# Both parts of a split weight in one tile, with a start offset chosen by each use

## The chip, the core and the metric

The kernel runs on one core of one Trainium2 chip. The metric is device time in microseconds (us) of that core, the median of several executions. The core has a matrix engine (TensorE, "PE" in the profile, its weight loads "PEld"), a vector engine (DVE), a scalar engine (ACT), GpSimd (POOL) and a queue for transfers (SP). The engines work from SBUF, which has 128 partitions; TensorE's results go to PSUM. An address in this text is a byte offset within a partition of SBUF.

## What is computed

One decoder layer for 512 tokens of width 2048: a norm, one wide projection, three groups of heads, an output projection added to x, and a last norm.

```python
h = rmsnorm(x, norm_g[l])
proj = h @ w_in[l]
(cv_a, cv_b, cv_gate, fq, fk, fv, f_logit, fox_gate,
 mq, mem_gate) = jnp.split(proj, SPLITS, axis=-1)
...
y_conv = (u @ w_conv_pw[l]) * jax.nn.silu(cv_gate)
...
y_fox = y_fox * jax.nn.silu(fox_gate)
...
y = jnp.concatenate([y_conv, y_fox, y_mem], axis=-1)
x = x + y @ w_out[l]
return rmsnorm(x, final_g)
```

The convolution group and the memory group have 512 channels each, the forgetting attention (fox) has 8 heads of 128. Keys and values of the memory group come from 256 memory tokens and `w_mem_kv`.

## The kernel before

**Products in parts.** Every float32 operand of a product is held as two parts, hi and lo, and a product is three matmuls: hi with hi, hi with lo, lo with hi (`mm3`, lines 102-106). `split` (line 90) makes the parts: ACT copies the source to hi (line 93), DVE subtracts hi from the source and writes lo (line 94).

**Weights.** A weight comes by DMA into a `raw` tile of 4096 bytes per partition (six buffers). `operand` (line 117) splits it into two tiles, `whi` and `wlo`, of 4096 bytes each, three buffers for each. A tile holds eight slices of 128 columns, 512 bytes apart, or two of 512 columns (2048 bytes apart), or four of 256 (1024 bytes apart). `weights` (line 126) does this for a whole weight, in two halves.

**Where a weight is used.** The operand that stays in the array is loaded by a weight load (the *stationary* operand, 128 columns); the other streams through it (the *moving* operand, 256 or 512 columns).

- Start, line 225: memory values. The weight moves, the memory rows `m_hi`, `m_lo` (`mh`, `ml`) are stationary. 512 columns.
- Start, lines 268-273: memory keys. The weight is stationary, `mh`, `ml` move. 256 columns.
- `project` (line 297): 128 features of the wide projection. The weight is stationary, the normed x (`hh`, `hl`) moves, 512 columns, 48 matmuls in a row. It is called 22 times: 8 for the convolution's inputs, 4 for its gates, 4 for the memory queries, 4 for the memory gates, 2 for the first pair of the fox heads.
- Lines 586-591: the convolution's pointwise product. The weight moves, `csh`, `csl` are stationary. 512 columns.
- `pair` (line 710): two blocks of 128 features by seven products of quarters. In `product` (line 727) the weight is stationary and a quarter of the normed x, or a sum of quarters (`s0`, `s1`, `s2`), moves, 256 columns, 24 matmuls for each product. 15 pairs are made so. Three results of a pair are kept in SBUF by ACT (`kept`, line 705, tags p1, p5 and u2, two buffers each) and read by DVE.
- `sides` (line 919), the output projection's plain part: the weight moves, the parts of y (`rs`) are stationary, 512 columns.
- `product` of the output projection (line 975), its part by quarters: the weight moves, `rh` is stationary, 256 columns.

**Order.** Instructions go to the engines in the order in which the program's scheduler sets them; each engine runs its own in order. Attention of one head runs between the products of the next pair, so that transposes and small products stand among the pair's matmuls.

**Addresses.** Tiles of pools on the left are laid out upwards, each rounded to 32 bytes; those on the right lie under the top. The constants stand first, then `raw`, `whi`, `wlo` (pool `wp`), then the pools of the stages.

| tiles | first address | modulo 512 |
|---|---|---|
| constants: ident, mean_r, half_neg, cols, cwt, bf_t, ccol, cb | 16512 | 128 |
| six `raw` | 20480 | 0 |
| three `whi`, three `wlo` | 45056, 57344 | 0 |
| first of a stage's pool on the left: `mh`, then `csh` | 69632 | 0 |
| normed x (`hh`, `hl`), later also the parts `rh` | 163808 | 480 |
| sums `s0` to `s2`, later the parts `rs` | 114656 | 480 |

A constant of few bytes takes a slot of 32: half_neg and bf_t have 4 bytes each and one slot each, cols has 176 bytes in a slot of 192.

Of the kernel before, what the change touches and what calls it, by code (L numbers as in the profile page):

```python
# [10 lines left out]
F32 = mybir.dt.float32  # L11
# [36 lines left out]
def hybrid_layer_kernel(  # L48
# [31 lines left out]
    def nm(s):  # L80
        uid[0] += 1
        return f"{s}_{uid[0]}"
# [7 lines left out]
    def split(hi, lo, src, scale=None):  # L90
        """hi + lo == src (times scale): twelve significant bits each."""
        if scale is None:
            ins = nc.scalar.copy(hi, src)  # L93
            nc.vector.tensor_tensor(lo, src, hi.bitcast(F32), ALU.subtract)  # L94
        else:
            ins = nc.scalar.activation(hi, src, AF.Identity, scale=scale)
            nc.vector.scalar_tensor_tensor(
                lo, src, scale, hi.bitcast(F32), ALU.mult, ALU.subtract
            )
        return ins.ins  # L100
# [15 lines left out]

    def operand(src, out=None):
        """src [P, n, c], whole -> its two parts."""
        if out is None:
            out = tuple(  # L120
                wp.tile(list(src.shape), F32R, tag=t, name=nm(t), bufs=3) for t in ("whi", "wlo")
            )
        split(*out, src)
        return out

    def weights(src, n, c, raw=None, hold=None):
        """src [n * P, c] -> k -> (hi, lo) of its k-th P rows."""
        half = n // 2
        src = src.rearrange("(k p) f -> p k f", p=P)
        parts = []  # L130
        for j in range(2):
            rows = slice(j * half, (j + 1) * half)
            r = raw_tile(half, c) if raw is None else raw[:, rows, :]
            nc.sync.dma_start(out=r, in_=src[:, rows, :])
            parts.append(operand(r, tuple(t[:, rows, :] for t in hold) if hold else None))
        return lambda k: tuple(t[:, k % half, :] for t in parts[k // half])

# [1 line left out]
    ident = const.tile([P, P], F32, name="ident")  # L139
    make_identity(nc, ident)  # L140
    mean_r = const.tile([P, P], F32R, name="mean_r")
    half_neg = const.tile([P, 1], F32, name="half_neg")
    nc.vector.memset(half_neg, -0.5)
    NROW = 2 * KT + 3 * (CW // P)
    cols = const.tile([P, NROW], F32, name="cols")
    cwt = const.tile([P, CW // P, TAPS], F32, name="cwt")
    bf_t = const.tile([NH, 1], F32, name="bf_t")
    ccol = const.tile([P, NT, NH], F32, name="ccol")
    cd = dr.tile([NH, S], F32, name="cd")

    ht = ctx.enter_context(tc.tile_pool(name="ht", bufs=1, side="right", reuse_waits="tile"))
    # x normed, [feature, token], two features' tiles in each
    hs_ = [
# [10 lines left out]

    # ---- start: memory values and keys (rows transposed as they come, their
    # norm applied to the results), x normed and transposed ----
    with tc.tile_pool(name="start", bufs=1) as st:
        m_hi = [st.tile([P, M], F32R, name=f"mh{k}") for k in range(KT)]
        m_lo = [st.tile([P, M], F32R, name=f"ml{k}") for k in range(KT)]
        mean_f = st.tile([P, P], F32, name="mean_f")  # L170
        nc.vector.memset(mean_f, 1.0 / CW)
# [77 lines left out]
        for t in range(MT):  # L249
            nc.vector.tensor_scalar(diag[:, t, :], ident, rsm[:, t : t + 1], None, ALU.mult)  # L250
            split(mv[0][:, t, :], mv[1][:, t, :], os_[t], scale=rsm[:, t : t + 1])
        ones = st.tile([P, P], F32, name="ones")
        nc.vector.memset(ones, 1.0)
        rbc = st.tile([P, M], F32, name="rbc")
        pt = at((P, NROW - KT))
        nc.tensor.transpose(pt, small, ident[: NROW - KT, : NROW - KT])
        nc.vector.tensor_copy(cols[:, KT:], pt)

# [8 lines left out]
        for h in range(NM):  # L267
            wk = weights(w_mem_kv[:, h * P : (h + 1) * P], KT, P)
            load_x(h)
            norm_x(h)  # L270
            o = pj((P, M))
            for k in range(KT):
                mm3(o, wk(k), (m_hi[k], m_lo[k]), k == 0, k == KT - 1)
                if h == NM - 1:
                    x_column(k)
            if h == 0:
                pt = at((P, M))
                for t in range(MT):
                    nc.tensor.matmul(
                        pt[:, t * P : (t + 1) * P], ones, diag[:, t, :], start=True, stop=True  # L280
                    )
                nc.vector.tensor_copy(rbc, pt)
            kt = st.tile([P, M], F32, tag="kt", name=nm("kt"), bufs=1)
            nc.vector.tensor_tensor(kt, o, rbc, ALU.mult)
            split(mk[0][:, h, :], mk[1][:, h, :], kt)
# [11 lines left out]
    def project(f0, per=0):  # L297
        """[P features from f0, tokens] in PSUM."""
        w = weights(w_in[:, f0 : f0 + P], KT, P)
        o = pj()  # L300
        for k in range(KT):
            mm3(o, w(k), (h_hi[k], h_lo[k]), k == 0, k == KT - 1)
        background(per)
        return o

    def silu_of(pool, o, tag, bufs):
        """silu of a PSUM tile."""
        sg = pool.tile([P, S], F32, tag=tag, name=nm(tag), bufs=bufs)
        nc.scalar.activation(sg, o, AF.Sigmoid)
        nc.vector.tensor_tensor(sg, o, sg, ALU.mult)  # L310
        return sg

# [1 line left out]
    NC = CW // P  # L314
    PAD = TAPS - 1
    with tc.tile_pool(name="conv", bufs=1, reuse_waits="tile") as cp:
# [151 lines left out]
        with tc.tile_pool(name="matt", bufs=1, reuse_waits="tile") as ma:  # L468
            # the channel norm's sums and the gates run between the heads
            gates = []  # L470
# [66 lines left out]

        # sums of h's quarters (token halves by feature halves); the last takes
        # the place of the quarter that no product needs
        spool = ctx.enter_context(  # L540
# [55 lines left out]

    # ---- the output projection's operands; what they need of the room of h and
    # its sums falls free with the last pair's products. The convolution's and
    # the memory's parts of y are multiplied as they are; the heads' parts by the
    # same form as the pairs, with sums of their quarters (token halves by halves  # L600
    # of the heads) ----
    NB = D // S
# [55 lines left out]
    def head_ys(j, fa, fb):  # L658
        """Heads j and 4 + j, whole: their quarters' parts and those of the
        sums, which take the room of fa and fb."""  # L660
        base = [room_h(w, j, (2, S)) for w in "hl"]
# [23 lines left out]

# [1 line left out]
    with tc.tile_pool(name="fox", bufs=1, reuse_waits="tile") as fx:  # L687
# [17 lines left out]
        def kept(src, tag):  # L705
            t = fx.tile([P, M], F32, tag=tag, name=nm(tag), bufs=2)
            nc.scalar.copy(t, src)
            return t

        def pair(fa, fb):  # L710
            """Features fa.. and fb.., P each, by Winograd's form of Strassen's
            seven products: the first in PSUM, by token halves, the second in
            SBUF. In three steps, for another pair's to come between."""
            HK = KT // 2
# [8 lines left out]

            # Sums are taken in PSUM: a product adds onto what its bank holds,
            # which copies and an addition have read or changed before. Only a
            # bank's first product starts afresh.
            def product(o, w, a, start=False):
# [159 lines left out]

# [1 line left out]
    head_ys(3, heads[6], last_y)  # L889
    with tc.tile_pool(name="outp", bufs=1, reuse_waits="tile") as op:  # L890
# [3 lines left out]
        gb = op.tile([P, D], F32, name="gb")  # L894
        # by token halves and column blocks
        res = [[op.tile([P, 2, S], F32, name=f"res{h}{n}") for n in range(NB)] for h in range(2)]
# [22 lines left out]
        def sides(n):  # L919
            """y's other parts; the last time, a token tile at a time and to the end."""  # L920
            final = n == NB - 1
# [11 lines left out]
            for j in range(4):  # L933
                hold = tuple(room_h(w, 2 + j, (2, S)) for w in "hl") if final and j >= 2 else None
                ws.append(operand(next_piece(), hold))
                if not final:
                    for t in range(NT):
                        tile_product(os_[t], j, t, ws[j])
                if j == 0:
                    yield  # L940
            for t in range(NT):
                if not final:
                    add(of(t, n), os_[t])
                    continue
                # the very last one by halves, for less to follow its products
                spans = [ALL] if t < NT - 1 else [slice(0, M), slice(M, S)]
# [28 lines left out]
        def product(o, w, name, start=False):  # L975
            wh, wl = operand(w)
            for k in range(HK):
# [102 lines left out]
```

## Time and profile before

| | us |
|---|---|
| median of 3 executions | 870.75 |
| lowest and highest | 870.74 and 870.83 |
| profiled execution, first to last instruction | 868.8 |

For the profiled execution only its span is shown; the median of the timed ones is 1.95 us above it, and that is taken as what lies around the span. In the profile "PE" is the time in which a matmul was under way. The length shown for one matmul is modelled and overlaps the next one's, so what a matmul costs is read from one start to the next. Rows of groups read: line, engine, operation, result and operands (moving first, then stationary), shapes, count, busy us, mean ns of one.

### The profile page before, as it was taken

The numbers are of one execution on the slowest core, as the hardware profiler recorded it, in microseconds if no ns is written. First come the engines' busy times: TensorE is split into PE (matmuls) and PEld (weight loads), VectorE is DVE, ScalarE is ACT, GpSimd is POOL, SyncE is SP. The second block draws the span as 40 slices with busy tenths as digits, with TensorE's granted clock in tenths as the row PEclk, the third lists the DMA queues.
The fourth block names the chain that finished last, engine by engine and source line by source line (L and its number), as shares of the span: only waits on it lengthen the run. The fifth ranks groups of instructions, "written<-read, shape, count | busy, mean of one in ns | idle before, by whom it ended". The sixth has DMA issues, their size and how long they took to land.

```text
span 868.8 us, 14045 instructions
## 1 busy us (share of the span) xinstructions
PE 855.3 (98%) x5562; PEld 775.1 (89%) x5562; DVE 704.8 (81%) x1051; ACT 436.2 (50%) x679; POOL 45.1 (5%) x76
## 2 busy tenths in 40 slices
PE   8999999999999999999999999999999999999996
PEld 6897887888888888999999999999999888998995
DVE  4686799999977998998787878878797886876964
ACT  4874322224346544566565555656464852443523
POOL 1011000000000002010101010101010000000001
PEclk9999999999999999999999999999999999999999
DMA  9972233333332333233434243333334627351415
GB/s 323 356 197 76 70 82 105 97 97 89 94 85 85 109 90 117 79 106 109 121 93 127 74 120 101 107 103 91 107 84 146 239 73 267 97 195 49 146 49 194
DMA packets 143265, 107.52 MB, mean 124 GB/s; under 512 B 3892, under 2 KB 126816, under 8 KB 142560
## 3 DMA queue, kind: packets, MB, share of 16 engines
q1 hardware_dynamic: 141696, 102.52, 39.3%
q0 software_dynamic: 1504, 4.11, 1.3%
q8 instruction: 43, 0.70, 0.3%
q14 instruction: 22, 0.18, 0.1%
HBM read 98.46 MB, written 8.14 MB: 123 GB/s over the span
## 4 chain that ended last, share of the span: by engine, by line
PE 95%; issue 1%; ACT 1%; DVE 1%; DMA 1%; SPq 0%; POOL 0%; POOLq 0%; ACTq 0%
PE pj L732 33%; PE pj L104 13%; PE pj L105 13%; PE pj L106 13%; PE pj L981 8%; PE at L104 3%; PE at L105 3%; PE at L106 3%; PE at L820 1%; DMA raw<-in_w_mem_kv_dram 1%; PE pj L409 0%; PE pj L408 0%; PE pj L262 0%; PE at L262 0%; PE at L782 0%
## 5 line engine op out<-in xcount | busy, mean ns | idle before, releaser
L93 ACT CAST whi<-raw 128x1024 fp32r<-128x1024 f32 x205 | 215.1, 1051 | 324.2 <-PE pj L105 110.9
L94 DVE TENSOR_TENSOR wlo<-raw,whi 128x1024 fp32r<-128x1024 f32 x205 | 250.1, 1221 | 87.5 <-ACT whi L93 86.6
L105 PE MATMUL pj<-hl,whi 128*128 128x512 f32 x352 | 139.6, 397 | 0.0
L106 PE MATMUL pj<-hh,wlo 128*128 128x512 f32 x352 | 139.1, 396 | 0.0
L104 PE MATMUL pj<-hh,whi 128*128 128x512 f32 x352 | 138.9, 396 | 0.0
L732 PE MATMUL pj<-hh,wlo 128*128 128x256 f32 x480 | 135.0, 281 | 0.0
L732 PE MATMUL pj<-hl,whi 128*128 128x256 f32 x480 | 134.9, 281 | 0.0
L732 PE MATMUL pj<-hh,whi 128*128 128x256 f32 x480 | 134.8, 281 | 0.0
L703 DVE TENSOR_TENSOR raw<-raw,raw 128x1024 f32<-128x1024 f32 x76 | 92.7, 1220 | 0.5
L732 PEld LDWEIGHTS pj<-hl,whi 128*128 128x128 f32 x480 | 90.4, 188 | 0.1
L732 PEld LDWEIGHTS pj<-hh,whi 128*128 128x128 f32 x480 | 90.5, 188 | 0.0
L732 PEld LDWEIGHTS pj<-hh,wlo 128*128 128x128 f32 x480 | 90.4, 188 | 0.0
L329 DVE SCALAR_TENSOR_TENSOR acc<-up,cwt,acc 128x512 f32<-128x512 f32 x120 | 85.2, 741 | 0.4
L981 PE MATMUL pj<-whi,rh 128*128 128x256 f32 x448 | 80.0, 280 | 0.7 <-DVE sst L1035 0.4
L104 PEld LDWEIGHTS pj<-hh,whi 128*128 128x128 f32 x352 | 66.1, 188 | 15.9 <-PE pj L262 0.2
L106 PEld LDWEIGHTS pj<-hh,wlo 128*128 128x128 f32 x352 | 66.1, 188 | 15.7
L105 PEld LDWEIGHTS pj<-hl,whi 128*128 128x128 f32 x352 | 66.1, 188 | 15.5
L981 PEld LDWEIGHTS pj<-whi,rh 128*128 128x128 f32 x448 | 68.8, 188 | 1.3 <-DVE res L907 1.1
L981 PE MATMUL pj<-wlo,rh 128*128 128x256 f32 x224 | 62.3, 279 | 0.0
L981 PEld LDWEIGHTS pj<-wlo,rh 128*128 128x128 f32 x224 | 42.1, 188 | 0.2
L796 POOL TENSOR_SCALAR_AFFINE_SELECT b<-b 128x128 f32<-128x128 f32 x32 | 21.3, 676 | 265.6 <-ACT b L795 234.0
L732 PE MATMUL pj<-s0h,whi 128*128 128x256 f32 x120 | 34.9, 291 | 0.0
(302 smaller groups left out, 1720.5 us busy)
## 6 DMA issues: line engine op xcount, KB each, us to landing
raw<-in_w_in_dram SPq DMA_DIRECT2D x104, 512.0 KB, 3.6
raw<-in_w_out_dram SPq DMA_DIRECT2D x32, 512.0 KB, 4.5
raw<-in_w_mem_kv_dram SPq DMA_DIRECT2D x12, 512.0 KB, 7.3
xr<-in_x_dram SPq DMA_DIRECT2D x4, 1024.0 KB, 7.8
res<-in_x_dram SPq DMA_DIRECT2D x8, 512.0 KB, 6.8
out_dram<-res SPq DMA_DIRECT2D x16, 256.0 KB, 2.8
rs<-yd SPq DMA_DIRECT2D x15, 256.0 KB, 4.6
mr<-in_mem_dram SPq DMA_DIRECT2D x8, 256.0 KB, 7.2
```

Source lines behind the costliest of these rows:

```text
L93: ins = nc.scalar.copy(hi, src)
L94: nc.vector.tensor_tensor(lo, src, hi.bitcast(F32), ALU.subtract)
L104: nc.tensor.matmul(o, ah, bh, start=start, stop=False)
L105: nc.tensor.matmul(o, ah, bl, start=False, stop=False)
L106: nc.tensor.matmul(o, al, bh, start=False, stop=stop)
L329: return lambda: nc.vector.scalar_tensor_tensor(a, up[:, j : j + S], cwt[:, c, j : j + 1], a, ALU.mult, ALU.add)
L703: nc.vector.tensor_tensor(o, p, q, ALU.subtract)
L732: nc.tensor.matmul(o, p[:, k, :], q, start=start and k == 0 and i == 0, stop=k == HK - 1 and i == 2, skip_group_check=True,)
L796: nc.gpsimd.affine_select(out=b[:, sl], in_=b[:, sl], pattern=[[-1, P]], compare_op=ALU.is_ge, fill=MASKED, base=0, channel_multiplier=1,)
L820: nc.tensor.transpose(tp[:, (i - j) * P : (i - j + 1) * P], pr[i][:, j * P : (j + 1) * P], ident)
L981: nc.tensor.matmul(o[:, m, :], p, q[:, k, :], start=start and k + m + i == 0, stop=k == HK - 1 and i == 2, skip_group_check=True,)
```

## The change

`operand` makes one tile `wb` of 8704 bytes (two pieces of 4096 and 512 to spare), three buffers, in place of a `whi` and a `wlo`. The two parts stand in it 4096 bytes apart, from an offset that the caller names: 0 (PAIRED), 8 elements or 32 bytes (EVEN), 16 elements or 64 bytes (HEADS). Without a name it is 0. The memory keys, `project` and `sides` name EVEN, the output projection's quarters name HEADS; the pairs, the memory values and the pointwise product keep 0. half_neg and bf_t become two further columns of `cols`; two constants of the start, mean_f and ones, share the buffer of `kt`; the kept results of a pair (p1, p5, u2) have one buffer each. The copy of the small rows into `cols` ends at column NROW.

```diff
+    PIECE = 8 * P
+    PAIRED, EVEN, HEADS = 0, 8, 16
+
+    def operand(src, out=None, off=0):
         if out is None:
+            both = wp.tile([P, 2 * PIECE + P], F32R, tag="wb", name=nm("wb"), bufs=3)
             out = tuple(
-                wp.tile(list(src.shape), F32R, tag=t, name=nm(t), bufs=3) for t in ("whi", "wlo")
+                both[:, o : o + PIECE].rearrange("p (n c) -> p n c", c=src.shape[2])
+                for o in (off, off + PIECE)
             )
         split(*out, src)
...
-    def weights(src, n, c, raw=None, hold=None):
+    def weights(src, n, c, raw=None, off=0):
...
-            parts.append(operand(r, tuple(t[:, rows, :] for t in hold) if hold else None))
+            parts.append(operand(r, off=off))
...
-    half_neg = const.tile([P, 1], F32, name="half_neg")
+    NROW = 2 * KT + 3 * (CW // P)
+    cols = const.tile([P, NROW + 2], F32, name="cols")
+    half_neg, bf_t = cols[:, NROW : NROW + 1], cols[:NH, NROW + 1 : NROW + 2]
     nc.vector.memset(half_neg, -0.5)
-    NROW = 2 * KT + 3 * (CW // P)
-    cols = const.tile([P, NROW], F32, name="cols")
     cwt = const.tile([P, CW // P, TAPS], F32, name="cwt")
-    bf_t = const.tile([NH, 1], F32, name="bf_t")
...
-        mean_f = st.tile([P, P], F32, name="mean_f")
+        mean_f = st.tile([P, M], F32, tag="kt", name="mean_f", bufs=1)[:, :P]
...
-        ones = st.tile([P, P], F32, name="ones")
+        ones = st.tile([P, M], F32, tag="kt", name="ones", bufs=1)[:, :P]
...
-            wk = weights(w_mem_kv[:, h * P : (h + 1) * P], KT, P)
+            wk = weights(w_mem_kv[:, h * P : (h + 1) * P], KT, P, off=EVEN)
...
-        w = weights(w_in[:, f0 : f0 + P], KT, P)
+        w = weights(w_in[:, f0 : f0 + P], KT, P, off=EVEN)
...
-            t = fx.tile([P, M], F32, tag=tag, name=nm(tag), bufs=2)
+            t = fx.tile([P, M], F32, tag=tag, name=nm(tag), bufs=1)
...
-                ws.append(operand(next_piece(), hold))
+                ws.append(operand(next_piece(), hold, EVEN))
...
-            wh, wl = operand(w)
+            wh, wl = operand(w, off=HEADS)
```

More of the change, by code (lines that the diff above doesn't have):

```diff
@@ L115, in raw_tile @@
         return wp.tile([P, n, c], F32, tag="raw", name=nm("raw"), bufs=6)
-    def operand(src, out=None):
+    PIECE = 8 * P
+    PAIRED, EVEN, HEADS = 0, 8, 16
+    def operand(src, out=None, off=0):
         if out is None:
+            both = wp.tile([P, 2 * PIECE + P], F32R, tag="wb", name=nm("wb"), bufs=3)
             out = tuple(
-                wp.tile(list(src.shape), F32R, tag=t, name=nm(t), bufs=3) for t in ("whi", "wlo")
+                both[:, o : o + PIECE].rearrange("p (n c) -> p n c", c=src.shape[2])
+                for o in (off, off + PIECE)
             )
@@ L256, in hybrid_layer_kernel @@
         nc.tensor.transpose(pt, small, ident[: NROW - KT, : NROW - KT])
-        nc.vector.tensor_copy(cols[:, KT:], pt)
+        nc.vector.tensor_copy(cols[:, KT:NROW], pt)
         def x_column(k):
```

## The prediction

> **What bounds the kernel now.** First the page: the span, the engines' shares, and the chain of work that ended last.
>
> ```profile
> span 868.8 us, 14045 instructions
> ...
> PE 855.3 (98%) x5562; PEld 775.1 (89%) x5562; DVE 704.8 (81%) x1051; ACT 436.2 (50%) x679; POOL 45.1 (5%) x76
> ...
> PEclk9999999999999999999999999999999999999999
> ...
> PE 95%; issue 1%; ACT 1%; DVE 1%; DMA 1%; SPq 0%; POOL 0%; POOLq 0%; ACTq 0%
> PE pj L732 33%; PE pj L104 13%; PE pj L105 13%; PE pj L106 13%; PE pj L981 8%; PE at L104 3%; PE at L105 3%; PE at L106 3%; PE at L820 1%; DMA raw<-in_w_mem_kv_dram 1%; PE pj L409 0%; PE pj L408 0%; PE pj L262 0%; PE at L262 0%; PE at L782 0%
> ```
>
> TensorE is never long idle, at full granted clock, and 95% of the chain is matmuls. Next, whom TensorE waits for (total us, times, longest), first and last of seven rows, and the stretches where DVE might be near:
>
> ```profile
> PE pj L104 <- ACT mh L96: 2.4, 1, 2.4
> ...
> PE pj L732 <- DVE wlo L94: 0.2, 1, 0.2
> ```
>
> ```profile
> 150.00:240.00 90.00, 90.00 (x408) 73.24 (x407) 83.09 (x127) 28.79 (x45) 0.58 (x1) 1.00 0.33 91
> ...
> 525.00:570.00 45.00, 45.00 (x375) 44.74 (x374) 37.58 (x56) 26.83 (x44) 2.83 (x5) 1.00 0.38 106
> ```
>
> TensorE waits for a few us in all. DVE (third busy time) has 6.9 of 90 us free in the convolution and 7.4 of 45 in a head's stage. So the time is the number of matmuls times the distance from one start to the next, and the change can only act through that distance, or by making an operand late.
>
> **The distance is not the same everywhere.** Rows of the timeline, 512 moving columns: `project` first, then the pointwise product, then `sides` with a weight moving, then the end of `sides`, where the weight lies in the room of h. Each fence has the first row of an unbroken stretch and the first row behind it.
>
> ```profile
> 98.06 0.40 PE L106 MATMUL pj<-hh,wlo 128*128 128x512 f32 x1
> ...
> 103.66 0.40 PE L106 MATMUL pj<-hh,wlo 128*128 128x512 f32 x1
> ```
>
> ```profile
> 315.41 0.39 PE L104 MATMUL pj<-csh,whi 128*128 128x512 f32 x1
> ...
> 326.31 0.40 PE L104 MATMUL pj<-hh,whi 128*128 128x512 f32 x1
> ```
>
> ```profile
> 787.09 0.40 PE L104 MATMUL pj<-whi,rs 128*128 128x512 f32 x1
> ...
> 792.69 0.40 PE L104 MATMUL pj<-whi,rs 128*128 128x512 f32 x1
> ```
>
> ```profile
> 845.98 0.39 PE L104 MATMUL pj<-rh,rs 128*128 128x512 f32 x1
> ...
> 848.72 0.40 PE L105 MATMUL at<-wlo,rs 128*128 128x512 f32 x1
> ```
>
> Distances: 5.60 us over 24 matmuls, **233.3 ns**; 10.90 over 48, **227.1**; 5.60 over 24, **233.3**; 2.74 over 12, **228.3**. Now 256 columns: pairs and quarters of the output projection as merged pieces of the chain (start, us, what), memory keys from the timeline.
>
> ```profile
> 518.77 13.84 PE pj L732 x117
> ...
> 736.31 14.01 PE pj L981 x120
> ```
>
> ```profile
> 47.01 0.28 PE L105 MATMUL pj<-ml,whi 128*128 128x256 f32 x1
> ...
> 48.45 0.28 PE L105 MATMUL pj<-ml,whi 128*128 128x256 f32 x1
> ```
>
> **118.3 ns** for a pair's matmul, **116.75** for the quarters, and 1.44 us over 12, **120.0**, for the keys. Put these beside the addresses. Let D be the stationary operand's address less the moving one's, modulo 512; slices of all these tiles lie multiples of 512 apart, so D is one number for a whole stage.
>
> | columns | D = 0 | D = +32 | D = -32 |
> |---|---|---|---|
> | 512 | 227.1 (csh, w), 228.3 (rh, rs) | 233.3 (`project`) | 233.3 (`sides`) |
> | 256 | 120.0 (keys) | 118.3 (pairs) | 116.75 (quarters) |
>
> The rows at the end of the pointwise product:
>
> ```profile
> 325.63 0.39 PE L104 MATMUL pj<-csh,whi 128*128 128x512 f32 x1
> 325.86 0.39 PE L105 MATMUL pj<-csl,whi 128*128 128x512 f32 x1
> 326.09 0.39 PE L106 MATMUL pj<-csh,wlo 128*128 128x512 f32 x1
> ```
>
> Starts here are 226 to 227 ns apart (0.68 us over three, with the row at 326.31 above): a stream at D = 0 settles at 226.7, and the mean of 227.1 holds a slow beginning. What could carry it shows where weight loads stand beside matmuls:
>
> ```profile
> 683.98 0.28 PE L732 MATMUL pj<-s2l,whi 128*128 128x256 f32 x1
> 683.98 0.19 PEld L732 LDWEIGHTS pj<-s2h,wlo 128*128 128x128 f32 x1
> ```
>
> The load for the next matmul begins with the matmul ahead of it, so two reads of SBUF run side by side. I choose to read D as the cause, because two quite different streams at D = 0 agree.
>
> **The change part by part.** Two slots of 32 bytes go from the constants (cols grows from 176 to 184 bytes, still 192), so `raw` begins at 20480 - 64 = 20416, `wb` at 20416 + 6 x 4096 = 44992, which is 448 modulo 512; 8704 is 17 x 512, so all three buffers are. With its offset a weight is at 448 (PAIRED), 480 (EVEN) or 0 (HEADS). Pools behind begin at 44992 + 3 x 8704 = 71104, also 448. Tiles on the right stay. Hence:
>
> - `project`: weight 480, h 480, D from +32 to 0.
> - `sides`: weight 480, y 480, D from -32 to 0.
> - pairs: weight 448, h and sums 480, D from +32 to -32.
> - keys: weight 480, `mh` 448, D from 0 to +32.
> - values, pointwise product, output quarters, the last `rh` weights: D as before.
>
> Counts are from the groups by shape; of like rows one stands for the others (three of 352, three of 56 and three of 52, three of 64; for the pairs three of 480 and nine of 120).
>
> ```profile
> L104 PE MATMUL pj<-hh,whi 128*128 128x512 f32 x352 | 138.9, 396 | 0.0
> ...
> L732 PE MATMUL pj<-hh,whi 128*128 128x256 f32 x480 | 134.8, 281 | 0.0
> ...
> L732 PE MATMUL pj<-s0h,whi 128*128 128x256 f32 x120 | 34.9, 291 | 0.0
> ...
> L104 PE MATMUL at<-whi,rs 128*128 128x512 f32 x56 | 20.8, 395 | 0.0
> ...
> L104 PE MATMUL pj<-whi,rs 128*128 128x512 f32 x52 | 20.0, 400 | 0.6 <-ACT whi L93 0.6
> L104 PE MATMUL pj<-mh,whi 128*128 128x256 f32 x64 | 18.8, 293 | 0.0
> ```
>
> 1. `project`: 1056 matmuls. 48 in a row, as in the pointwise product, so its 227.1, settling included: 1056 x 6.2 = **6.5 us**. Bounds: 0, and 6.6 ns each (7.0) if settled throughout.
> 2. `sides`: 324 matmuls, in runs broken by output quarters, so the short run's 228.3: 324 x 5.0 = **1.6 us**. Bounds 0 and 2.1.
> 3. Pairs: 15 x 7 x 24 = 2520 matmuls, 118.3 - 116.75 = 1.54 ns each: **3.9 us**. The trace has no pair at D = -32; the quarters are its nearest row (same columns, same order of parts). Bounds: 120.0, the dearest row of 256 columns, a loss of 4.3; and 3.9.
> 4. Keys: 192 matmuls from 120.0 to the pairs' 118.3: **0.3 us**.
> 5. Smaller products whose tiles shift by 64 bytes against the right side (memory attention, forget logits: some 100 matmuls) get a D that no long stream here shows. At 3 ns each either way that is 0.3 us; I take 0.
>
> Nothing is added to an engine: the same copies and subtractions are made. The kept results lose a buffer. In ACT's and DVE's timelines:
>
> ```profile
> 469.25 0.39 ACT L707 COPY p<-pj 128x256 f32<-128x256 f32 x1
> ...
> 491.71 0.36 ACT L707 COPY p<-pj 128x256 f32<-128x256 f32 x1
> ```
>
> ```profile
> 482.12 0.41 DVE L700 TENSOR_TENSOR col<-pj,p 128x256 f32<-128x256 f32 x1
> ```
>
> p5, written at 469.25, is last read by 482.53, and the next pair's copy comes at 491.71: 9.2 us to spare, so the second buffer is worth nothing. If that cover went, ACT's queue behind the copy (a pair's next hi copies) would wait, and TensorE with it. The hi part's slot now comes free only with the lo part's last matmul, one matmul (0.12 or 0.23 us) later. DVE's and TensorE's rows show the lead of an operand, here the shortest in this head's stage:
>
> ```profile
> 497.39 1.21 DVE L94 TENSOR_TENSOR wlo<-raw,whi 128x1024 fp32r<-128x1024 f32 x1
> ```
>
> ```profile
> 500.58 0.28 PE L732 MATMUL pj<-s2h,wlo 128*128 128x256 f32 x1
> ```
>
> 500.58 - 498.60 = 1.98 us, sixteen matmuls, so I cost it at 0. TensorE's saving is 12.3 us, 1.4%: DVE's 83.1 us then stand in 88 us instead of 90, still with room. The constants that share `kt` are written before the stage's waits begin; nothing there. Sum: 6.5 + 1.6 + 3.9 + 0.3 = **12.3 us**. The span goes from 868.8 to 856.5; with the 1.95 us between span and median, 858.4.
>
> **A rule against it.** The streams above differ by 6 ns of 233 with D while the weight load runs beside the matmul. The Trainium skill (TensorE: Matmul & The Clock Gate, Step-by-step: what each phase is for) says that TensorE has two independent read ports into SBUF and that "Loading the next tile's weights doesn't steal SBUF read bandwidth from the running matmul." By that rule no address could matter, the sum would be 0 and the time 870.75; the trace's 227.1 beside 233.3 does not agree with it.
>
> **Rivals.**
>
> - *D is not the cause.* The fast streams would owe their distance to something else: where the results go, what other engines do. For: the D = 0 sample of 512 columns is only some 100 quiet matmuls. Against: two stages with different neighbours agree, and so does the reversed order at 256 columns. Time: 870.7. This is also the case in which the change does not do what it says. The page's rule above would have it so. Chance 7%.
> - *Only the 512-column streams gain.* The quarters' 116.75 might belong to their results, which go to two halves of a bank by turns, not to D. Then 12.3 - 3.9 = 8.4 us, 862.3. Chance 10%.
> - *The pairs land on the keys' level*, 120.0: 8.4 - 4.3 = 4.1 us, 866.6. Chance 2%.
> - *Operands come late: slower.* One tile frees both parts together, so each hi copy starts a matmul later. Were there no lead, each operand would hold TensorE for that: 105 of pairs x 0.12, 60 of 512 columns (44 of `project`, 16 of `sides`) x 0.23, 28 of the quarters x 0.12 = 29.8 us, less the 12.3: 888. It decides where an operand's lead falls under one matmul; with 1.98 us in the rows it would need ACT or DVE to lag by a whole subtraction more. Chance 4%.
> - Forecast as summed, 858.4: 77%.
>
> **How the numbers follow.** The likeliest is 858.4. Its own uncertainty is the settling of broken streams (up to 2 us less gain) and a different order of instructions among attention and pairs (1 to 2 us either way); the only sure further gain is 0.5 + 0.5 us from settled streams in steps 1 and 2. With the second rival taken in, the range is 856.0 to 863.0. Faster or slower by 0.2% (1.7 us) is about what a measurement of this kernel can tell from no change: faster 0.77 + 0.10 + 0.02 = 0.89, same 0.07, slower 0.04.
>
> **What would show it.** In the timeline after, `project` should run at 227 ns a matmul once settled and `sides` near 228; a chain piece of L732 should have 116.7 ns for each matmul (117 in 13.66 us, not 13.84); L981 should stay at 116.75, and the keys leave 120. DVE and ACT copies should keep their length. I am wrong if `project` stays at 233, if L732 stays at 118 or rises, or if TensorE's list of waits gains rows for hi or lo parts.

## The result and the profile after

| | before | after |
|---|---|---|
| median, us (4 executions each) | 870.76 | 860.78 |
| lowest and highest | 870.74, 870.83 | 860.14, 860.89 |
| span of the profiled execution | 868.8 | 859.0 |

The ratio is 0.9883, with a 95% interval from 0.9869 to 0.9897: 10.0 us less, where 12.3 were forecast (858.4 us). The profiled execution took 860.89 us, 1.9 us more than its span, as before.

First a correction. The text ahead of the prediction says that in the convolution's pointwise product the weight moves and `csh`, `csl` are stationary. It is the other way round, as the rows show (the moving operand stands first): `csh` and `csl` move. D is 0 either way, and no number hangs on it.

The page of after: span, busy times, granted clock in tenths over 40 slices, and the chain by engine (in the rows further on, line 732 is now 739 and 981 is 988).

```profile
span 859.0 us, 14010 instructions
...
PE 844.9 (98%) x5562; PEld 773.0 (90%) x5562; DVE 703.7 (82%) x1051; ACT 435.6 (51%) x679; POOL 46.6 (5%) x76
...
PEclk8999999999999999999999999999999999999999
...
PE 95%; ACT 2%; issue 1%; DVE 1%; DMA 1%; SPq 0%; POOL 0%; ACTq 0%; POOLq 0%
```

The same 5562 matmuls still fill 98% of a shorter span, and DVE and ACT are busy as long as before; of the granted clock, only the first of 40 slices is lower (8, where before had 9). So the time went out of the distance from matmul to matmul. Timeline rows of after, `project` and then `sides`, each a matmul and the 24th behind it:

```profile
118.05 0.39 PE L104 MATMUL pj<-hh,wb 128*128 128x512 f32 x1
...
123.49 0.39 PE L104 MATMUL pj<-hh,wb 128*128 128x512 f32 x1
```

```profile
777.70 0.39 PE L104 MATMUL pj<-wb,rs 128*128 128x512 f32 x1
...
783.14 0.39 PE L104 MATMUL pj<-wb,rs 128*128 128x512 f32 x1
```

Both are 5.44 us over 24: 226.7 ns, where the same stages had 233.3. Now merged pieces of the chain of after, three of the pairs and one of the quarters (start, us, what):

```profile
395.78 13.66 PE pj L739 x117
...
421.84 13.90 PE pj L739 x118
...
440.96 13.31 PE pj L739 x114
...
727.04 14.02 PE pj L988 x120
```

Per matmul: 116.75, 117.8, 116.75 and 116.8 ns. The first and third are the forecast's level; the second is a level between that and the 118.3 of before. The memory keys in the timeline, a matmul and the 21st behind it:

```profile
46.85 0.28 PE L105 MATMUL pj<-ml,wb 128*128 128x256 f32 x1
...
49.33 0.28 PE L105 MATMUL pj<-ml,wb 128*128 128x256 f32 x1
```

2.48 us over 21, 118.1 ns, where it was 120.0. All distances added up from start to start, over the whole trace, by class:

| matmuls | before, us | after, us | difference | forecast |
|---|---|---|---|---|
| `project`, 1056 | 247.31 | 241.12 | -6.19 | -6.5 |
| `sides`, 324 | 75.97 | 74.29 | -1.68 | -1.6 |
| pairs, 2520 | 302.18 | 299.51 | -2.67 | -3.9 |
| memory keys, 192 | 23.98 | 23.76 | -0.22 | -0.3 |
| quarters, 672 | 79.74 | 79.89 | +0.15 | 0 |
| memory values, 96 | 24.91 | 26.05 | +1.14 | 0 |
| transposes, 266 | 29.30 | 28.71 | -0.59 | 0 |
| attention, 264 | 42.17 | 42.36 | +0.19 | 0 |

The first four rows give 10.76 of the 12.3 us; the lower four take 0.89 back. What is left, 9.87, is the span's 9.8. Last, whom TensorE waits for in after (total us, times, longest), whole:

```profile
PE pj L104 <- ACT mh L96: 2.3, 1, 2.3
PE at L184 <- POOL ident masks.py:199: 1.4, 1, 1.4
PE pj L104 <- ACT wb L93: 1.2, 1, 1.2
PE pj L988 <- DVE res L914: 0.7, 2, 0.4
PE at L241 <- DMA mr<-in_mem_dram: 0.4, 1, 0.4
```

No weight of `project` or of a pair is in it. The one row for a weight is at the turn from the fox heads to the output projection, a single wait of 1.2 us where before had one of 0.6 there (`ACT whi L93`) and one of 0.2 for a pair's `wlo` just ahead. In the table it lies in the row of pairs, since it follows the last pair's last matmul, and takes some 0.2 us from their gain.

### The profile page after: what moved, and what is told of

It is laid out like the page before. It is cut to its first block, busy times and chain, and to the rows that moved or that the text cites. A ratio compares the mean times of both kernels' runs of the same rounds, so it can differ in the third digit from the quotient of the medians.

```text
span 859.0 us, 14010 instructions
## 1 busy us (share of the span) xinstructions
PE 844.9 (98%) x5562; PEld 773.0 (90%) x5562; DVE 703.7 (82%) x1051; ACT 435.6 (51%) x679; POOL 46.6 (5%) x76
## 4 chain that ended last, share of the span: by engine, by line
PE 95%; ACT 2%; issue 1%; DVE 1%; DMA 1%; SPq 0%; POOL 0%; ACTq 0%; POOLq 0%
PE pj L739 33%; PE pj L104 13%; PE pj L105 13%; PE pj L106 13%; PE pj L988 8%; PE at L104 3%; PE at L105 3%; PE at L106 3%; PE at L827 1%; DMA raw<-in_w_mem_kv_dram 1%; ACT wb L93 0%; PE pj L415 0%; PE pj L416 0%; PE pj L269 0%; PE at L789 0%
## 5 line engine op out<-in xcount | busy, mean ns | idle before, releaser
L93 ACT CAST wb<-raw 128x1024 fp32r<-128x1024 f32 x205 | 215.4, 1052 | 246.1 <-PE pj L106 73.2
L94 DVE TENSOR_TENSOR wb<-raw,wb 128x1024 fp32r<-128x1024 f32 x205 | 250.0, 1221 | 64.2 <-ACT wb L93 60.3
L739 PE MATMUL pj<-hh,wb 128*128 128x256 f32 x960 | 177.3, 280 | 0.0
L739 PEld LDWEIGHTS pj<-hh,wb 128*128 128x128 f32 x960 | 150.1, 188 | 0.0
L104 PE MATMUL pj<-hh,wb 128*128 128x512 f32 x352 | 137.3, 391 | 0.1
L105 PE MATMUL pj<-hl,wb 128*128 128x512 f32 x352 | 137.4, 391 | 0.0
L106 PE MATMUL pj<-hh,wb 128*128 128x512 f32 x352 | 137.2, 390 | 0.0
L739 PE MATMUL pj<-hl,wb 128*128 128x256 f32 x480 | 134.2, 280 | 0.0
L739 PEld LDWEIGHTS pj<-hl,wb 128*128 128x128 f32 x480 | 90.2, 188 | 0.0
L988 PE MATMUL pj<-wb,rh 128*128 128x256 f32 x672 | 80.2, 280 | 0.7 <-DVE res L914 0.7
L988 PEld LDWEIGHTS pj<-wb,rh 128*128 128x128 f32 x672 | 79.5, 188 | 1.4 <-DVE res L914 1.1
L104 PEld LDWEIGHTS pj<-hh,wb 128*128 128x128 f32 x352 | 66.1, 188 | 14.0 <-PE pj L269 0.3
L106 PEld LDWEIGHTS pj<-hh,wb 128*128 128x128 f32 x352 | 66.1, 188 | 13.7
L105 PEld LDWEIGHTS pj<-hl,wb 128*128 128x128 f32 x352 | 66.1, 188 | 13.5
```

Source lines behind the costliest of these rows:

```text
L104: nc.tensor.matmul(o, ah, bh, start=start, stop=False)
L105: nc.tensor.matmul(o, ah, bl, start=False, stop=False)
L106: nc.tensor.matmul(o, al, bh, start=False, stop=stop)
L739: nc.tensor.matmul(o, p[:, k, :], q, start=start and k == 0 and i == 0, stop=k == HK - 1 and i == 2, skip_group_check=True,)
L988: nc.tensor.matmul(o[:, m, :], p, q[:, k, :], start=start and k + m + i == 0, stop=k == HK - 1 and i == 2, skip_group_check=True,)
```

## The experiments

Each edit below is made to the kernel after the change, except where it says the kernel before. "Settled" is the mean distance in a run of matmuls of equal D, without its first nine. Each timed kernel has its own executions of the kernel before beside it; they had medians of 870.6 to 871.1.

### Is it D, or the rest of the change?

The rest first: one tile, moved constants, single buffers for kept results, but all offsets equal, so that D of `project`, `sides` and the pairs is again that of before.

```diff
-    PAIRED, EVEN, HEADS = 0, 8, 16
+    PAIRED, EVEN, HEADS = 16, 16, 16
...
-    def operand(src, out=None, off=0):
+    def operand(src, out=None, off=PAIRED):
...
-    def weights(src, n, c, raw=None, off=0):
+    def weights(src, n, c, raw=None, off=PAIRED):
```

> The changed kernel with one offset of 64 bytes for every weight: the merged tile, the moved constants and the single buffers of the kept results stay, but weights lie at 0 modulo 512 and h at 480, as before, so D is +32 for project and the pairs and -32 for sides and the output quarters. If D alone sets the spacing: project 233.3 ns, pairs 118.3 ns, time 870 to 871.5 us, no change against before. If the merged tile or another order of instructions brought part of the gain, the time lies below 869 us.

Measured: 870.91 us (10 executions), ratio 0.9998 (0.9989 to 1.0007). `project` took 247.35 us and the pairs 302.08, as before. Two small stages do move here, since weights and the tiles behind them shift against each other: the keys get D = +64 and the pointwise product too, 23.14 us and 11.21 (before 23.98 and 10.90). Pieces of the pairs in this kernel's chain:

```profile
402.01 13.85 PE pj L739 x117
...
428.35 13.96 PE pj L739 x118
```

They are 118.4 and 118.3 ns, the level of before. The wait at the turn to the output projection is 1.1 us here, so its growth comes with the one tile and not with D. The second kernel goes the other way: the kernel before, with its two tiles and two buffers, and 448 bytes more in the constants, which put `whi` and `wlo` at 448 modulo 512. D of pairs becomes -32 and D of quarters +32; `project` and `sides` swap their signs, -32 and +32.

```diff
-    cols = const.tile([P, NROW], F32, name="cols")
+    cols = const.tile([P, NROW + 112], F32, name="cols")
...
-        nc.vector.tensor_copy(cols[:, KT:], pt)
+        nc.vector.tensor_copy(cols[:, KT:NROW], pt)
```

> The kernel before with 448 bytes of spare constants and nothing else: its separate tiles lie at 448. D: project -32, pairs -32, sides +32, output quarters +32, keys 0. If D is the cause, the pairs go from 118.3 to 116.9 ns (about 3 us less, as measured for the change), the quarters from 116.75 to 118.3 (1 us more), project and sides stay at 233.3: 868.0 to 869.5 us. If the pairs gained from the merged tile, nothing falls: 870.7 or, with the quarters' loss, 871.8.

Measured: 868.88 us (8 executions), ratio 0.9975 (0.9965 to 0.9986). Its chain, a piece of pairs and one of quarters:

```profile
427.36 13.66 PE pj L732 x117
...
732.68 14.21 PE pj L981 x120
```

These pairs run at 116.75 ns (some short runs at 117.8) and the quarters at 118.4, an exchange of the two levels of before (118.3 and 116.75). Pairs fall from 302.18 to 298.92 us, quarters rise from 79.74 to 80.56, and `project` and `sides` stay to the hundredth (247.31 and 75.97). Moving the weights and the pools behind them by 448 bytes, with no instruction changed but the length of a copy's target, moves the time. Together the two kernels show that the offset acts, and that the tile, the constants and the buffers together are worth nothing that 0.1% could show.

### Where the slower start comes from

The memory values lost 1.14 us. One suspect is `raw`, which now begins at 448 modulo 512; here it is back at a multiple of 512, and so is `wb`, with offsets that keep each named D but that of the keys, which becomes -32.

```diff
-    PAIRED, EVEN, HEADS = 0, 8, 16
+    PAIRED, EVEN, HEADS = 112, 120, 0
...
-    cols = const.tile([P, NROW + 2], F32, name="cols")
+    cols = const.tile([P, NROW + 18], F32, name="cols")
...
-            wh, wl = operand(w)
+            wh, wl = operand(w, off=PAIRED)
```

> The changed kernel with 64 bytes of spare constants, so that raw, wb and the stages' pools begin at 0 modulo 512 again, and offsets of 448, 480 and 0 that keep every D of the change (the memory keys go from +32 to -32). If the slower start of the changed kernel (memory values 26.0 us in place of 24.9, transfer packets of 512 bytes at 33 ns in place of 27 in the first 40 us) comes from raw tiles at 448, it returns to 27 ns and the time falls by about 1 us more for the start and 0.3 for the keys, to 859.5. If it is chance between executions, the time stays at 860.5 to 861 (0.3 less for the keys).

Measured: 859.88 us (4 executions), ratio 0.9869 (0.9855 to 0.9884), which overlaps with the change's own interval. The memory values still took 25.94 us. Packets of 512 bytes in the first 40 us did get shorter, 27.4 ns in the mean against 33 in the kernel after (27.1 before), but the values gained nothing, so that suspect falls. The table of windows shows what stands beside the loss (us, then busy us and matmuls of PE, PEld, DVE, ACT, POOL, granted clock, DMA share, GB/s): 10 to 15 us in before, in after, and in this kernel.

```profile
10.00:15.00 5.00, 5.00 (x21) 4.02 (x21) 3.81 (x6) 2.36 (x4) 0.00 (x0) 0.73 1.06 408
```

```profile
10.00:15.00 5.00, 5.00 (x14) 3.89 (x14) 3.68 (x6) 2.04 (x3) 0.00 (x0) 0.50 1.05 389
```

```profile
10.00:15.00 5.00, 5.00 (x14) 3.85 (x14) 3.98 (x7) 2.21 (x3) 0.00 (x0) 0.50 1.05 407
```

Where TensorE was granted half of its clock it did 14 matmuls in these 5 us; at 0.73 it did 21. In the half-clock stretch most of the values' matmuls stand 427 ns apart, behind it some 230. The later kernel with D = 256 and +64 (below) has the same instructions and addresses in this stage as the kernel after, and its profile shows this:

```profile
10.00:15.00 5.00, 5.00 (x22) 3.98 (x21) 4.07 (x7) 2.62 (x4) 0.00 (x0) 0.77 1.05 389
```

Its values took 24.61 us. So the 1.14 us are not the change's doing: like kernels had 24.6 and 26.05 by the clock that they were granted. The distances are the surer sign: the kernel with one tile and the old offsets shows a granted clock of 1.00 in these 5 us, yet its matmuls stand 427 ns apart up to 13.8 us. Why one execution is granted more than another was not tried.

### How the distance depends on D

To see the relation whole, each of the 22 calls of `project` and each of the 15 pairs got its own D (at_d turns a D into an offset in elements).

```diff
+PROJ_D = (0, 64, 96, 128, 160, 192, 224, 256, 288, 320, 352, 384, 416, 448, 16, 8, 4, 496, 504, 508, 48, 464)
+PAIR_D = (64, 96, 128, 160, 192, 224, 256, 288, 320, 352, 384, 416, 448, 16, 496)
...
+    at_d = lambda d: (d + 32) % 512 // 4
+    proj_off = deque(at_d(d) for d in PROJ_D)
...
-        w = weights(w_in[:, f0 : f0 + P], KT, P, off=EVEN)
+        w = weights(w_in[:, f0 : f0 + P], KT, P, off=proj_off.popleft())
...
-                wh, wl = operand(w)
+                wh, wl = operand(w, off=off)
```

> Each call of project and each pair takes its own offset, so that D runs through 0 to 480 in steps of 32, with a few finer ones, in one execution. If D modulo 512 is a relation between two reads that run side by side, the spacing is a smooth or stepped function of D with 226.7 at 0 and 233.3 at +32 and -32 for 512 columns, and 116.7 at -32 for 256. If D = 0 and D = -32 are special only by chance, the spacing shows no order in D. A D that is better than those of the change would show below 226.7 or below 116.7.

The same with a finer choice:

```diff
+PROJ_D = (256, 252, 248, 244, 240, 260, 264, 272, 276, 280, 12, 16, 20, 24, 500, 496, 488, 184, 192, 200, 208, 72)
+PAIR_D = (64, 56, 72, 48, 80, 60, 68, 52, 320, 216, 232, 220, 228, 224, 40)
```

> As the scan by 32, with finer steps: project at 256 and 4 to 24 bytes around it, at 12 to 24, near -16, and at 184 to 208; pairs at +64 and 4 to 24 around it, at 320 and at 216 to 232. If the relation has a period of 256, 240 and 272 give what -16 and 16 gave (settled 228.5 and 226.7 ns), 248 and 264 what -8 and 8 gave (233.3 and 230.6). If the period is 512, they differ. A level under 226.7 or 116.6 would be a better place for the operands.

Measured: 867.4 and 868.11 us, one execution each; most of their streams run at a slow D. Settled distances at 512 columns, each D beside the one 256 bytes on:

| D and ns | D + 256 and ns |
|---|---|
| 0: 226.7 in the kernel after; 227.2 and 229.2 in the first scan's first call, in short runs | 256: 226.7 |
| 4: 232.3 | 260: 232.4 |
| 8: 230.6 | 264: 230.7 |
| 16: 226.7 in one kernel, 233.4 in the other | 272: 233.4 |
| 64: 233.4 | 320: 233.4 |
| 96: 234.2 | 352: 234.2 |
| 192: 228.9 | 448: 229.0 |
| 240: 228.3 | 496: 228.5 and 227.7 |
| 244: 233.3 | 500: 233.3 |
| 252: 226.7 | 508: 226.7 |

Timeline rows behind two of these, D = 256 in the first scan (5.44 us over 24) and D = 260 in the second (5.59 us over 24):

```profile
156.44 0.39 PE L108 MATMUL pj<-hh,wb 128*128 128x512 f32 x1
...
161.88 0.39 PE L108 MATMUL pj<-hh,wb 128*128 128x512 f32 x1
```

```profile
134.00 0.40 PE L108 MATMUL pj<-hh,wb 128*128 128x512 f32 x1
...
139.59 0.39 PE L108 MATMUL pj<-hh,wb 128*128 128x512 f32 x1
```

Four bytes more than 256 cost 6 ns a matmul; four bytes less cost nothing. The relation returns after 256 bytes, not after 512, and no D went below 226.7. In the scans only the weight moves, so by them alone its own address could be what counts. The pointwise product decides that: with the weight at 0 and `csh` at 0 it settled at 226.7 ns in the kernel before; with the weight at 0 and `csh` at 448 (D = +64), in the kernel with one tile and the old offsets, it took this for 24 matmuls:

```profile
317.21 0.39 PE L104 MATMUL pj<-csh,wb 128*128 128x512 f32 x1
...
322.81 0.39 PE L104 MATMUL pj<-csh,wb 128*128 128x512 f32 x1
```

That is 5.60 us, 233.3 ns, the level of D = 64 in the scan: it is the distance between the two operands that counts. At 256 columns the levels reach from 113.4 to 120.4 ns: D = 64 had 113.4 in the second scan and 116.6 in the first, 320 had 116.9, 52 had 116.8, 192 and 448 both 117.8, 160 and 416 both 120. For D = 64 the chains of the two kernels show it in the same first pair, first scan and then second:

```profile
347.13 11.31 PE pj L747 x96
```

```profile
347.99 10.89 PE pj L747 x96
```

117.8 and 113.4 ns, with the same operands and addresses, but another D in the `project` calls ahead. So D doesn't fix the distance alone; a stream can settle at more than one level.

### Is there a better D?

The scans offer +64 for the pairs, and 256 in place of 0 for `project` and `sides`:

```diff
-        w = weights(w_in[:, f0 : f0 + P], KT, P, off=EVEN)
+        w = weights(w_in[:, f0 : f0 + P], KT, P, off=72)
...
-                wh, wl = operand(w)
+                wh, wl = operand(w, off=24)
...
-                ws.append(operand(next_piece(), hold, EVEN))
+                ws.append(operand(next_piece(), hold, 72))
```

> The changed kernel with other offsets: project and sides at D = 256 in place of 0, pairs at D = +64 in place of -32; all else as in the change. In the scan, D = 256 stood at 226.7 ns from its second matmul on and +64 at 116.6. If the relation has a period of 256 bytes, D = 256 is the same as 0 and settles as slowly: project stays at 228.3 ns on average, and only the pairs can gain, from 117.1 to 116.6 (1.3 us): 859.5. If D = 256 settles at once, project and sides gain some 1.5 us more: 858. If +64 was good by chance of its place in the scan, the pairs stay at 117.1 and the time at 860.8.

Measured: **856.10 us** (4 executions), ratio 0.9835 (0.9819 to 0.9852), whole below the change's interval. `project` took 241.09 us and `sides` 74.33: D = 256 is D = 0. The pairs took 295.82, 3.7 us less than with -32, and their chain has both levels again, 117.8 and 113.4 ns:

```profile
438.93 13.43 PE pj L739 x114
...
464.67 13.38 PE pj L739 x118
```

The profiled span fell by 4.9 us (859.0 to 854.1): 3.7 are the pairs', and 1.4 those of the values of the start (24.61 against 26.05), which are not the edit's; other stages lost 0.2. In the next kernel `project` and `sides` got the D = 16 that had run at 226.7 in the first scan, with pairs at +64 (offsets 12, 4 and 24 for the calls of the diff above).

> The changed kernel with project and sides at D = 16 in place of 0 and pairs at +64 in place of -32. In the scan D = 16 settled at 226.7 ns, as 0 does. If broken streams settle sooner there, project falls under 228.3 ns on average and the time under 859.5; if 16 is the same as 0, 859.5 by the pairs alone; if settling hangs on chance, project spreads to 230 and the time is 860 to 861.

Measured: 863.26 us (4 executions), ratio 0.9915 (0.9901 to 0.993). `project` took 246.54 us, 233.5 ns in the mean, and `sides` 75.45: the fast D = 16 of the scan was a matter of its place. The call that had run at 226.7 ns there did so again (227.0), and so did the second call, 226.7; nearly all others settled at 233. The pairs kept their gain (295.41). The last kernel for the time: the fastest so far, and +64 at the keys and the quarters also.

```diff
-            wk = weights(w_mem_kv[:, h * P : (h + 1) * P], KT, P, off=EVEN)
+            wk = weights(w_mem_kv[:, h * P : (h + 1) * P], KT, P, off=16)
...
-            wh, wl = operand(w, off=HEADS)
+            wh, wl = operand(w, off=120)
```

> The kernel of e5 (project and sides at D = 256, pairs at +64) with the output quarters and the memory keys at +64 too, in place of -32 and +32. If +64 is the better place for any stream of 256 columns, the quarters fall from 116.8 to about 115.5 ns and the keys from 118.3 to 115.5: 672 x 1.3 + 192 x 2.8 = 1.4 us, 854.7. If it is good only for the pairs' order of results, the time stays at 856.1.

Measured: 855.87 us (4 executions), ratio 0.9826 (0.981 to 0.9843). Quarters went from 79.77 to 79.05 us and keys from 23.76 to 23.29: 1.2 us of the 1.4 that were expected. The time shows little of it, since the values of the start took 25.54 us in the profiled execution, against 24.61. Against the kernel with pairs alone at +64 the intervals overlap, so the two can't be told apart; both beat the change.

### Which meeting is the costly one?

If one reading of a tile collided with one loading, giving the hi and the lo part of a `project` weight different D should slow one place of the three matmuls only. By turns hi had 0 and lo 244, and hi -12 and lo 0 (`low` is the lo part's own offset).

```diff
+    turns = deque([(8, 69), (5, 8)])
...
-        w = weights(w_in[:, f0 : f0 + P], KT, P, off=EVEN)
+        hi_off, lo_off = turns[0]
+        turns.rotate(1)
+        w = weights(w_in[:, f0 : f0 + P], KT, P, off=hi_off, low=lo_off)
```

> The changed kernel with the two parts of project's weights at different D, by turns: one call with hi at 0 and lo at 244, the next with hi at -12 and lo at 0 (alone, 0 settles at 226.7 ns, 244 and -12 stand at 233.3). Matmuls run hi, hi, lo, and a load runs beside the matmul ahead of it. If the load beside a matmul is what it meets, the distance behind the second matmul (lo is loaded beside it) differs from the others in each call: the long one in the first kind of call, the short one in the second. If a matmul's own stationary operand counts, it is the third. If the distances do not hang on single meetings but on the state of the whole stream, no place stands out.

Measured: 860.51 us, one execution. Mean distances behind the first, second and third matmul of `mm3`: 227.7, 228.2 and 227.5 ns in one kind, 227.5, 228.8 and 228.7 in the other. These means mix two sorts of calls. Fourteen of the 22, of both kinds, settled at 226.7 to 226.8, as this one with hi at -12 and lo at 0:

```profile
110.20 0.39 PE L104 MATMUL pj<-hh,wb 128*128 128x512 f32 x1
...
115.64 0.39 PE L104 MATMUL pj<-hh,wb 128*128 128x512 f32 x1
```

Five settled at 231 to 232. In triples that took 690 to 705 ns the places differ: 232.1, 234.6 and 230.9 ns in the first kind, 229.7, 233.4 and 233.5 in the second. A long second place in the first kind fits "the load beside a matmul", a short first place in the second kind fits neither reading. So the same two D give a fast or a slow stream, and the 233.3 that -12 (500 or 244) gave where both parts had it is not a price of single matmuls: the distance seems to hang on the state of the whole stream. What collides inside the chip these runs don't settle: that stays open.

## Why the prediction was right, and where its sizes were off

- **What bounds the kernel** was read rightly: with no engine's work changed, 10 us went out of matmul distances, and TensorE's share stayed at 98%.
- **D is the cause:** right. The tile without the offsets gave 870.91 us, and the offset without the tile gave 868.88. The rival by which D does nothing, 870.7, falls. The Trainium skill (TensorE: Matmul & The Clock Gate, Step-by-step: what each phase is for) says that loading the next weights takes no read bandwidth from the running matmul. As the prediction read that rule, 860.78 and 870.91 us, from kernels that differ in the offsets, would have to be one time; that reading doesn't hold here, though no run shows that read bandwidth is what is lost.
- **Modulo 512** was too much said: three values of D could not show a period. The scans show 256.
- **`project` and `sides`:** 6.19 and 1.68 us for 6.5 and 1.6. Both settle at the 226.7 named; `project`'s mean was 228.3, not 227.1 (before, 234.2 and not 233.3), since some of its 22 calls are broken by other work and settle anew.
- **Pairs** are the mis-sized term: 2.67 us for 3.9. The step took the quarters' 116.75 for every pair's matmul. The pairs settle at two levels, 116.75 and 117.8, and matmuls in undisturbed runs had 117.1 in the mean: that is some 1.0 of the 1.2 us that are missing, and the longer wait at the turn is the other 0.2. The 116.75 was true of quarters and of the kernel before moved by 448 (3.26 us there), so D = -32 can give it; the stream in the new kernel does so in some of its pieces only. With the weights' base at 0 and the same D the pairs took 298.75 us, so the level depends on more than D.
- **Keys and quarters:** as forecast (118.4 and 116.8 ns settled). The keys' D became +32, as worked out.
- **Single buffers and later slots at nothing:** nearly right. No wait for a part of a pair's or `project`'s weight came, and the change without its D lost nothing clear of noise, so the rival of late operands falls. But the wait at the turn grew from 0.6 and 0.2 us to 1.2, and to 1.1 with the one tile and the old D; the kernel before moved by 448 bytes still had 0.6 and 0.3. The sum had no term for it.
- **Only 512 columns gain** falls: the kernel before moved by 448 gained 2.2 us with `project` unchanged. Pairs on the keys' level falls too.
- **The start** was not in the sum: 1.1 us lost in the profiled execution to a lower granted clock, which other kernels with the same start did not lose.

The forecast's 12.3 less 1.5 (the four terms: 1.2 from pairs, 0.3 from `project`) less 0.9 (the rest of the table) is 9.9; the span fell by 9.8. The direction rested on two streams at D = 0 that agreed; the size of the 256-column term rested on one other stage, and that is the one that was off.

## What to carry to other kernels

When TensorE is the bound and its matmuls follow one another without gaps, compare the start-to-start distance of stages with the same shape: a difference of 2 or 3% between them may be the distance between the two operands' addresses and can be had by an offset alone, with no instruction changed. Try the offset by a scan within one kernel, one value for each call, and confirm the best in a kernel that uses it throughout, since a value that was fast at one place (16 here) can be slow at most others. Use a level from another stage as a bound, not as a price.

## What the runs showed of the hardware that was not expected

- The distance repeats with 256 bytes of D, and 4 bytes can matter: 226.7 ns at 252 and 256, 232.4 at 260 (512 columns).
- Equal addresses are among the best for 512 columns but not for 256: there +64 reached 113.4 ns, +32 118.3, and 256 (the same as 0) 120.0.
- A stream settles at one of several levels with the same D: 113.4 and 117.8 ns within one kernel's pairs.
- From 10 to 15 us the granted clock of like programs was 0.50 or 0.77, worth some 1.4 us of memory values.
